# A state-space layer on one core: carried products split by real and imaginary part, states kept in the scan's rows

## The chip, the cores and the metric

The kernel runs on one core of a Trainium2 chip. The metric is device time in microseconds (us) of one execution, lower is better. TensorE (PE in the profile) does the matrix products, VectorE (DVE) and ScalarE (ACT) the work on elements, GpSimd (POOL) some element work and the issue of part of the DMAs, and SyncE's queue (SPq) issues the loads of weights and tables.

## The reference

A trunk of two layers on 256 tokens of 2048 channels in float32: a convolution module, an MLP, a state-space layer with a gated output, a second MLP, a final norm. The change is in the state-space layer. It has 128 groups of 16 channels, each with 64 complex states:

```
bu_re = jnp.einsum("blgc,gpc->blgp", u, bb_re)     # input to the 64 states of each group
bu_im = jnp.einsum("blgc,gpc->blgp", u, bb_im)
_, _, s_re, s_im = lax.associative_scan(combine, (a_re, a_im, bu_re, bu_im), axis=1)
y = (jnp.einsum("blgp,gcp->blgc", s_re, c_re) - jnp.einsum("blgp,gcp->blgc", s_im, c_im))
y = gelu(y + d_skip * h)
z = y @ w_glu                                       # then val * sigmoid(gate)
```

## The kernel before

Nearly all the time is the five large dense products, in which every weight is split into a high and a low part: ScalarE writes `hi` (line 118), VectorE `lo` (line 125, on GpSimd for some steps), and TensorE does three products of each (lines 199 to 234). One step loads a block of weights (`raw`, line 92, on SyncE's queue, in the order of the steps), splits it in two halves up to four halves ahead, and multiplies. A half of the gated output's product is 12 matmuls of 512 columns.

The state-space layer is worked in chunks of 8 tokens. Four blocks B of 512 channels (32 groups) pass through these stages, for each block:

- `ssm_front` and `ssm_turn` (lines 1242 to 1272): products of the chunk's inputs with table W, and a transpose, so that the scan's rows are 128: 64 states of an even group (rows 0 to 63) and of the odd group beside it (rows 64 to 127).
- `ssm_scan` and `ssm_forth` (lines 1274 to 1310): on VectorE, turn the complex recurrence into two real scans, scan over the 32 chunks, and multiply by the turning factors R, which leaves four products in `S`.
- `ssm_states` (lines 1312 to 1320): the four products become the states `SS`, real part in rows 0 to 63 and imaginary part in rows 64 to 127, four VectorE operations on 64 rows each, since the halves change rows.
- `ssm_local` (lines 1322 to 1336): products with table M for what a chunk's own tokens give, `mv` in PSUM. Each matmul gives 32 of the 128 output rows (chunks of one quarter q), so four matmuls of four quarters stand beside each other in the array.
- `ssm_carry` (lines 1338 to 1351): products with table V (128 rows by 128 columns for each group) add what the state at a chunk's start gives: 32 matmuls a block, each of which runs as two instructions in the profile. ScalarE's Gelu then writes `y`.
- `ssm_out` (lines 1353 to 1366): transposes of `y` and the split into `yT`, the operand of the gated output's product.

Block 0 has all of this ahead of the first matmul of the gated output's product (`begin` in `glu`); blocks 1 to 3 are hung on steps of that product by a table of step numbers (`todo`), so their products stand between its matmuls on TensorE, and their VectorE work between the splits. The first block's parts of `ssm_local` for block 1 stand on both sides of `ssm_out(0)`.

Table V is made long before, as background work in the first MLP: `vstage(k)` (lines 1091 to 1105) makes it for 8 groups on VectorE in one buffer `bv` and stores it with one DMA on GpSimd's queue to `Vd` in DRAM; `kstage(k)` makes table K from the same buffer and stores it with four DMAs, `mstage` spreads K to M. `table` (lines 1183 to 1193) later fetches V of one block in two DMAs of 16 groups each, on SyncE's queue, in the order of the weight loads (`before_load`). Instructions of each engine are put into order by a scheduler with a model of its own; anchors (`behind`) fix some of that order.

Of the kernel before, what the change touches and what calls it, by code (L numbers as in the profile page):

```python
# [18 lines left out]
P = 128  # L19
# [8 lines left out]
G, ST, GC = 128, 64, 16  # L28
CH = 8
VW = PAD + T + 2  # L30
NQ = 4
# [5 lines left out]
class Trunk:  # L37
# [823 lines left out]
    def ssm_prep(self):  # L861
        nc, a, bg = self.nc, self.a, self.bg
# [2 lines left out]
        self.Wd = self.dram.tile([P, G, P], F32, name="Wd")  # L865
        self.Kd = self.dram.tile([G, GC, 15 * GC], F32, name="Kd")
        self.Md = self.dram.tile([P, G, P], F32, name="Md")
        self.Vd = self.dram.tile([P, G, P], F32, name="Vd")
        self.Bd = self.dram.tile([G, 2, ST, GC], F32, name="Bd")
        self.Rd = self.dram.tile([P, NQ, 1024], F32, name="Rd")  # L870
        self.xs = self.dram.tile([T, D], F32, name="xs")
        dma = nc.gpsimd.dma_start
# [221 lines left out]
        def vstage(k):  # L1094
            vs = s["bv"][:, 1, 0:1152].rearrange("p (g d c) -> p g d c", d=9, c=GC)
            g = slice(8 * k, 8 * k + 8)
            c = [s["c12"][:, i, g, :].unsqueeze(2).broadcast_to([P, 8, 8, GC]) for i in range(2)]
            p = [s[x][:, g, :].unsqueeze(3).broadcast_to([P, 8, 8, GC]) for x in ("pr", "pi")]
            t = self.t4([P, 8, 8, GC], name="vt")
            v = vs[:, :, 1:9, :]  # L1100
            self.tt(v, c[0], p[0], ALU.mult)
            self.tt(t, c[1], p[1], ALU.mult)
            self.tt(v, v, t, ALU.add)
            nc.scalar.activation(vs[:, :, 0, :], s["c12"][:, 0, g, :], AF.Copy)
            dma(out=self.Vd[:, g, :], in_=v.rearrange("p g d c -> p g (d c)"))

        def kstage(k):
            vs = s["bv"][:, 1, 0:1152].rearrange("p (g x) -> p g x", x=9 * GC)
# [74 lines left out]
    def table(self, kind, B):  # L1183

        if kind == "R":
            t = self.t4([P, 2, 16, 32], name="R") if B != 2 else self.S[:, 1]
            self.fetch(t.rearrange("p i g j -> p (i g j)"), self.Rd[:, B])
        else:
            t = self.blk_tile([P, 32, P], name=kind + "t")
            src = {"W": self.Wd, "M": self.Md, "V": self.Vd}[kind]  # L1190
            for h in range(0, 32, 16):
                self.fetch(t[:, h:h + 16, :], src[:, 32 * B + h:32 * B + h + 16, :])
        self.tables[kind, B] = t

    def ssm_block(self, b):
# [79 lines left out]
    def ssm_scan(self, B, first=None):  # L1275

        nc = self.nc
        ps, R = self.X.pop(B), self.tables["R", B]
        S, t = self.S[:, 0], self.S[:, 2:4]
        m = self.t2([P, 16, 32], name="m")  # L1280
        with self.behind(self.pow_ins):
            nc.gpsimd.memset(m[:, :, 0], 0.0)
        with self.behind(self.xev0 if B == 0 else self.uev):
            nc.scalar.activation(m[:, :, 1:32], self.m8[:, 16 * B:16 * B + 16].unsqueeze(2).broadcast_to([P, 16, 31]), AF.Copy)
        ps = [p.rearrange("p g q j -> p q g j")[:, :, :, 0:31] for p in ps]
        re = lambda x: x.rearrange("p (q g) j -> p q g j", q=NQ)[:, :, :, 1:32]
        c, s = re(R[:, 0]), re(R[:, 1])
        t1, t2 = re(t[:, 0, 0]), re(t[:, 1, 0])
        self.tt(re(S[:, 0]), c, ps[0], ALU.mult)
        self.tt(t1, s, ps[1], ALU.mult)  # L1290
        self.tt(re(S[:, 1]), c, ps[1], ALU.mult)
        self.tt(t2, s, ps[0], ALU.mult)
        self.tt(re(S[:, 0]), re(S[:, 0]), t1, ALU.add)
        self.tt(re(S[:, 1]), re(S[:, 1]), t2, ALU.subtract)
        flat = lambda x: x.rearrange("p g j -> p (g j)")
# [16 lines left out]
    def ssm_states(self, B):  # L1312
        nc = self.nc
        t = self.S[:, 2:4]
        SS = self.t4([P, 16, 2, 32], name="SS")
        for h in range(2):
            r = slice(64 * h, 64 * h + 64)
            self.tt(SS[0:64, :, h, :], t[r, 0, 0], t[r, 1, 1], ALU.subtract)
            self.scaled = nc.vector.tensor_tensor(out=SS[64:128, :, h, :], in0=t[r, 0, 1], in1=t[r, 1, 0], op=ALU.add)
        self.SS[B] = SS  # L1320

    def ssm_local(self, B, g0=0, g1=8):

        nc = self.nc
        M = self.tables["M", B]
        if B == 0:
            A = self.mv[B] = [self.bank([P, 4, CH, GC], name="mv"),
                              self.acc2()[:, 0].rearrange("p (g t c) -> p g t c", g=4, c=GC)]
        else:
            A = self.mv.setdefault(B, [])  # L1330
            A.extend(self.bank([P, 4, CH, GC], name="mv") for _ in range(g0 // 4, g1 // 4))
        U = self.xJ[:, B]
        for g in range(g0, g1):
            for q in range(NQ):
                self.mmm = nc.tensor.matmul(A[g // 4][32 * q:32 * q + 32, g % 4], lhsT=U[:, g, 32 * q:32 * q + 32],
                                 rhs=M[:, 8 * q + g, :], start=g % 4 == 0, stop=False, skip_group_check=True)

    def ssm_carry(self, B):

        nc = self.nc  # L1340
        SS = self.SS.pop(B)
        V = self.tables.pop(("V", B))
        A = self.mv.pop(B)
        for g in (0, 2, 4, 6, 1, 3, 5, 7):
            for q in range(NQ):
                self.vmm = nc.tensor.matmul(A[g // 4][32 * q:32 * q + 32, g % 4], lhsT=SS[:, 4 * q + g // 2, g % 2, :],
                                            rhs=V[:, 8 * q + g, :], start=False, stop=g % 4 == 3, skip_group_check=True)
        y = self.y = self.t4([P, CH, 8, GC], name="y")
        for g, t in (((0, slice(0, CH)), (4, slice(0, CH // 2)), (4, slice(CH // 2, CH))) if B == 0 else
                     ((0, slice(0, CH)), (4, slice(0, CH)))):  # L1350
            nc.scalar.activation(y[:, t, g:g + 4, :].rearrange("p t g c -> p g t c"), A[g // 4][:, :, t], AF.Gelu_apprx_tanh)

    def ssm_out(self, B):
        nc = self.nc
# [12 lines left out]
    def glu(self):  # L1367
# [6 lines left out]
        def begin():  # L1374
            self.mv, self.SS = {}, {}
            self.ssm_start()
# [231 lines left out]
```

## Time and profile before

| | us |
|---|---|
| time, median of 3 runs | 1987.38 (1987.24 to 1987.9) |
| profiled execution | 1987.61 |
| its span, first to last instruction | 1985.8 |
| TensorE busy | 1966.9 (99%) |
| VectorE busy | 1401.3 (71%) |
| ScalarE busy | 952.4 (48%) |
| GpSimd busy | 274.8 (14%) |
| granted TensorE clock, mean | 0.999 of full speed (2.4 GHz) |

The profiled execution is 0.23 us above the median, and 1.8 us of it lie outside the span. The share of busy time says that TensorE sets the time nearly everywhere; what another engine costs is found in the few places where TensorE waits, and what a change of TensorE's own work costs shows wherever it doesn't.

### The profile page before, as it was taken

How to read it: one execution, taken by the hardware profiler on the slowest of the kernel's cores; microseconds unless marked ns; L12 is line 12 of the kernel's file. 1: busy time of each engine (PE TensorE's matmuls, PEld its weight loads, DVE VectorE, ACT ScalarE, POOL GpSimd, SP SyncE). 2: the span in 40 equal slices, each digit the busy share in tenths (PEclk: the TensorE clock that was granted, in tenths of full speed). 3: DMA queues.
4: the chain of work that ended last, by engine and by line, in shares of the span. 5: the costliest groups of instructions: out<-in, count | busy, mean ns of one | idle time of the engine just before them, and what ended most of it. 6: DMA issues, size and time to landing. Idle time of an engine off the chain costs nothing.

```text
span 1985.8 us, 28885 instructions
## 1 busy us (share of the span) xinstructions
PE 1966.9 (99%) x11604; PEld 1687.0 (85%) x11604; DVE 1401.3 (71%) x1904; ACT 952.4 (48%) x1179; POOL 274.8 (14%) x252
## 2 busy tenths in 40 slices
PE   8999999999999999999999999999999999999998
PEld 8999788888888888888888788888888888888887
DVE  6899798888787777777558847565555565555655
ACT  6443655544444544444445445454444454444444
POOL 3998300000000221222010000000000000000000
PEclk9999999999999999999999999999999999999999
DMA  8767458667686877877898865665666656565653
GB/s 228 190 184 207 147 183 267 206 226 245 200 260 192 214 229 253 265 246 238 319 308 298 304 215 186 191 191 189 193 190 192 190 191 191 190 213 190 192 191 128
DMA packets 317030, 428.49 MB, mean 216 GB/s; under 512 B 9761, under 2 KB 211553, under 8 KB 313537
## 3 DMA queue, kind: packets, MB, share of 16 engines
q1 hardware_dynamic: 300976, 384.59, 61.6%
q0 software_dynamic: 12352, 37.49, 6.3%
q10 hardware_dynamic: 3568, 4.56, 0.8%
q8 instruction: 91, 1.49, 0.3%
q14 instruction: 43, 0.35, 0.1%
HBM read 400.08 MB, written 34.91 MB: 219 GB/s over the span
## 4 chain that ended last, share of the span: by engine, by line
PE 96%; DVE 2%; DMA 1%; issue 0%; SPq 0%; POOL 0%; ACT 0%; POOLq 0%; DVEq 0%; ACTq 0%
PE acc L199 24%; PE acc L222 15%; PE acc L223 15%; PE acc L224 15%; PE acc L202 12%; PE acc L213 3%; PE acc L212 3%; PE acc L211 3%; PE pk L484 1%; DMA Vt<-Vd 0%; SPq L92 0%; PE kp L1113 0%; PE xw L1254 0%; DMA raw<-in_conv_w_in_dram 0%; PE xt L254 0%
## 5 line engine op out<-in xcount | busy, mean ns | idle before, releaser
L118 ACT ACTIVATE hi<-raw 128x1024 fp32r<-128x1024 f32 x672 | 711.6, 1060 | 953.5 <-PE acc L224 510.2
L125 DVE TENSOR_TENSOR lo<-raw,hi 128x1024 fp32r<-128x1024 f32 x611 | 747.9, 1226 | 505.6 <-ACT hi L118 501.3
L199 PE MATMUL acc<-hT,hi 128*128 128x512 f32 x2048 | 514.4, 393 | 0.0
L199 PEld LDWEIGHTS acc<-hT,hi 128*128 128x128 f32 x2048 | 368.9, 189 | 68.0 <-issue 1.6
L222 PE MATMUL acc<-hi,rT 128*128 128x512 f32 x992 | 387.2, 391 | 0.0
L223 PE MATMUL acc<-lo,rT 128*128 128x512 f32 x992 | 386.4, 390 | 0.0
L224 PE MATMUL acc<-hi,rT 128*128 128x512 f32 x992 | 386.0, 389 | 0.0
L202 PEld LDWEIGHTS acc<-hT,lo 128*128 128x128 f32 x2048 | 279.6, 190 | 20.0
L202 PE MATMUL acc<-hT,lo 128*128 128x256 f32 x2048 | 286.3, 282 | 0.0
L222 PEld LDWEIGHTS acc<-hi,rT 128*128 128x128 f32 x992 | 186.3, 188 | 39.6 <-issue 1.6
L224 PEld LDWEIGHTS acc<-hi,rT 128*128 128x128 f32 x992 | 186.3, 188 | 39.1
L223 PEld LDWEIGHTS acc<-lo,rT 128*128 128x128 f32 x992 | 186.3, 188 | 38.0 <-issue 0.2
L125 POOL TENSOR_TENSOR lo<-raw,hi 128x1024 fp32r<-128x1024 f32 x60 | 143.1, 2402 | 31.3 <-ACT hi L118 24.8
L211 PE MATMUL acc<-hT,hi 128*128 128x256 f32 x512 | 146.1, 286 | 0.9 <-ACT hi L118 0.9
L212 PE MATMUL acc<-hT,hi 128*128 128x256 f32 x512 | 145.7, 286 | 0.3 <-DVE hT L259 0.3
L213 PE MATMUL acc<-hT,lo 128*128 128x256 f32 x512 | 145.5, 286 | 0.0
L829 DVE SCALAR_TENSOR_TENSOR cv<-vT,dw,cv 128x256 f32<-128x256 f32 x348 | 141.3, 486 | 2.2 <-ACT cv L527 1.7
L820 DVE TENSOR_TENSOR x<-x,acc 128x1024 f32<-128x1024 f32 (+1 forms) x72 | 83.6, 1161 | 27.6 <-PE acc L224 22.0
L211 PEld LDWEIGHTS acc<-hT,hi 128*128 128x128 f32 x512 | 98.9, 193 | 3.0 <-issue 1.6
L222 PE MATMUL acc<-hi,yT 128*128 128x512 f32 x256 | 101.1, 395 | 0.0
L212 PEld LDWEIGHTS acc<-hT,hi 128*128 128x128 f32 x512 | 98.8, 193 | 2.2 <-issue 1.6
L223 PE MATMUL acc<-lo,yT 128*128 128x512 f32 x256 | 99.9, 390 | 0.6 <-DVE lo L125 0.6
(285 smaller groups left out, 1722.9 us busy)
## 6 DMA issues: line engine op xcount, KB each, us to landing
raw<-in_mlp_w_up_dram SPq DMA_DIRECT2D x128, 1024.0 KB, 5.8
raw<-in_mlp_w_down_dram SPq DMA_DIRECT2D x128, 1024.0 KB, 5.2
raw<-in_ssm_w_glu_dram SPq DMA_DIRECT2D x32, 1024.0 KB, 5.5
raw<-in_conv_w_in_dram SPq DMA_DIRECT2D x60, 512.0 KB, 5.6
raw<-in_conv_w_out_dram SPq DMA_DIRECT2D x16, 1024.0 KB, 5.2
Vd<-bv POOLq DMA_DIRECT2D x16, 512.0 KB, 6.3
Md<-Kd POOLq DMA_DIRECT2D x32, 256.0 KB, 7.2
Wt<-Wd SPq DMA_DIRECT2D x8, 1024.0 KB, 10.1
```

The source lines that it names most:

```text
L118: self.nc.scalar.activation(hi, sl, AF.Copy)
L125: ins = eng.tensor_tensor(out=lo, in0=sl, in1=hi.bitcast(F32), op=ALU.subtract)
L199: mm(accs[m], lhsT=hi[:, kk, cs[m]], rhs=xT(k0 + kk), start=first and kk == 0, stop=False)
L202: mm(accs[m][:, 0:T], lhsT=lo[:, kk, cs[m]], rhs=xT(k0 + kk)[:, 0, :], start=False, stop=last and kk == 3)
L211: mm(accs[m], lhsT=hi[:, kk, c], rhs=x[:, 0, :], start=first and kk == 0, stop=False)
L212: mm(accs[m], lhsT=hi[:, kk, c], rhs=x[:, 1, :], start=False, stop=False)
L213: mm(accs[m], lhsT=lo[:, kk, c], rhs=x[:, 0, :], start=False, stop=last and kk == 3)
L222: mm(acc[:, b, :], lhsT=ak[:, 0, t], rhs=hi[:, kk, :], start=first and kk == 0, stop=False)
L223: mm(acc[:, b, :], lhsT=ak[:, 0, t], rhs=lo[:, kk, :], start=False, stop=False)
L224: self.mm_last = mm(acc[:, b, :], lhsT=ak[:, 1, t], rhs=hi[:, kk, :], start=False, stop=last and kk == 1)
L820: return self.nc.vector.tensor_tensor(out=out, in0=a, in1=b, op=op)
L829: return self.nc.vector.scalar_tensor_tensor(out=out, in0=a, scalar=s, in1=b, op0=op0, op1=op1)
```

## The change

- `ssm_states`: two VectorE operations on 128 rows in place of four on 64 rows. The states stay in the scan's rows: even groups in rows 0 to 63, odd groups in rows 64 to 127; `SS[:, 0]` is the real part, `SS[:, 1]` the imaginary part.
- `ssm_carry`: for each group and quarter two matmuls of 64 rows, one with the real and one with the imaginary part, in place of one of 128 rows: 64 matmuls a block. First the real products, even and odd groups in turn, then the imaginary ones, the four even groups and after them the four odd ones.
- Banks by parity: the even groups of a block accumulate in one PSUM bank and the odd ones in the other (before: groups 0 to 3 and 4 to 7). `ssm_local` walks the groups in that order, and each Gelu writes every second group of `y`.
- Table V is stored in these rows: `Vd` has, for each block, the real and the imaginary half, and `vstage` stores 8 groups with four DMAs of 64 rows by 4 groups. `table` fetches the real half with the first DMA and the imaginary half with the second.

```diff
-        self.Vd = self.dram.tile([P, G, P], F32, name="Vd")
+        self.Vd = self.dram.tile([P, NQ, 2, 16, P], F32, name="Vd")
...
-            dma(out=self.Vd[:, g, :], in_=v.rearrange("p g d c -> p g (d c)"))
+            for h in range(2):
+                for i in range(2):
+                    dma(out=self.Vd[64 * h:64 * h + 64, k // NQ, i, 4 * (k % NQ):4 * (k % NQ) + 4, :],
+                        in_=v[64 * i:64 * i + 64, h::2].rearrange("p g d c -> p g (d c)"))
...
-            src = {"W": self.Wd, "M": self.Md, "V": self.Vd}[kind]
             for h in range(0, 32, 16):
-                self.fetch(t[:, h:h + 16, :], src[:, 32 * B + h:32 * B + h + 16, :])
+                src = self.Vd[:, B, h // 16] if kind == "V" else {"W": self.Wd, "M": self.Md}[kind][:, 32 * B + h:32 * B + h + 16, :]
+                self.fetch(t[:, h:h + 16, :], src)
...
-        SS = self.t4([P, 16, 2, 32], name="SS")
-        for h in range(2):
-            r = slice(64 * h, 64 * h + 64)
-            self.tt(SS[0:64, :, h, :], t[r, 0, 0], t[r, 1, 1], ALU.subtract)
-            self.scaled = nc.vector.tensor_tensor(out=SS[64:128, :, h, :], in0=t[r, 0, 1], in1=t[r, 1, 0], op=ALU.add)
+        SS = self.t4([P, 2, 16, 32], name="SS")
+        self.tt(SS[:, 0], t[:, 0, 0], t[:, 1, 1], ALU.subtract)
+        self.scaled = nc.vector.tensor_tensor(out=SS[:, 1], in0=t[:, 0, 1], in1=t[:, 1, 0], op=ALU.add)
...
+    def ssm_group(self, A, i):
+        g = 2 * (i % 4) + i // 4
+        return g, A[i // 4][:, i % 4]
...
-        for g in (0, 2, 4, 6, 1, 3, 5, 7):
-            for q in range(NQ):
-                self.vmm = nc.tensor.matmul(A[g // 4][32 * q:32 * q + 32, g % 4], lhsT=SS[:, 4 * q + g // 2, g % 2, :],
-                                            rhs=V[:, 8 * q + g, :], start=False, stop=g % 4 == 3, skip_group_check=True)
...
+        def products(part, i):
+            g, out = self.ssm_group(A, i)
+            r = slice(64 * (g % 2), 64 * (g % 2) + 64)
             for q in range(NQ):
+                k = 4 * q + g // 2
+                self.vmm = nc.tensor.matmul(out[32 * q:32 * q + 32], lhsT=SS[r, part, k, :], rhs=V[r, 16 * part + k, :],
+                                            start=False, stop=part == 1 and i % 4 == 3, skip_group_check=True)
+        for i in (0, 4, 1, 5, 2, 6, 3, 7):
+            products(0, i)
+        for i in range(8):
+            products(1, i)
```

TensorE at block 0's carried products. Before, from the second pass over the two banks on (the pair of rows at the top stands twice); `mv` and `acc` are the two banks, x8 are matmuls:

```order
L1346 MATMUL mv_9958<-Vt_9448,SS_10045 32x128 x8
L1346 MATMUL acc_9959<-Vt_9448,SS_10045 32x128 x8
L1335 MATMUL mv_10086<-Mt_9946,xJ_9516 32x128 x16
L1359 MATMUL yt_10104<-ident_95,y_10082 128x128 x4
L1359 MATMUL yt_10105<-ident_95,y_10082 128x128 x4
```

The same place of the changed kernel (the pair of x4 rows at the top stands four times: these are the real products):

```order
L1358 MATMUL mv_10006<-Vt_9496,SS_10093 32x128 x4
L1358 MATMUL acc_10007<-Vt_9496,SS_10093 32x128 x4
L1358 MATMUL mv_10006<-Vt_9496,SS_10093 32x128 x16
L1358 MATMUL acc_10007<-Vt_9496,SS_10093 32x128 x16
L1342 MATMUL mv_10164<-Mt_9994,xJ_9564 32x128 x16
L1374 MATMUL yt_10182<-ident_95,y_10096 128x128 x4
```

Nothing moves past anything here: 32 matmuls on two banks by fours, then 32 that fill one bank after the other, stand where 32 stood.

VectorE at block 1's states, between `ssm_forth(1)` and the splits of the gated output's weights (`lo`) and the scaling of block 2's inputs (`xJ`). Before (the pair of `SS` rows stands twice):

```order
L820 TENSOR_TENSOR SS_10148<-S_9846 64x16x32
L1319 TENSOR_TENSOR SS_10148<-S_9846 64x16x32
L125 TENSOR_TENSOR lo_10154<-raw_9698,hi_10153 128x1024
L125 TENSOR_TENSOR lo_10174<-raw_9749,hi_10173 128x1024
L820 TENSOR_TENSOR xJ_9516<-xJ_9516,rJ_9839 128x512 x2
L125 TENSOR_TENSOR lo_10192<-raw_9749,hi_10191 128x1024
```

Now:

```order
L820 TENSOR_TENSOR SS_10226<-S_9894 128x512
L1320 TENSOR_TENSOR SS_10226<-S_9894 128x512
L125 TENSOR_TENSOR lo_10230<-raw_9746,hi_10229 128x1024
L820 TENSOR_TENSOR xJ_9564<-xJ_9564,rJ_9887 128x512 x2
L125 TENSOR_TENSOR lo_10250<-raw_9797,hi_10249 128x1024
L125 TENSOR_TENSOR lo_10268<-raw_9797,hi_10267 128x1024
```

Two operations are gone, and the scaling of block 2 stands ahead of one split more.

GpSimd's queue in the first MLP, at the stores of tables V and K. Before:

```order
L1105 DMA Vd<-bv 128x8x128 x2
L1121 DMA Kd<-ks 16x2x128 x8
L1124 DMA Md<-Kd 16x32x128 x7
L1105 DMA Vd<-bv 128x8x128
L1124 DMA Md<-Kd 16x32x128
```

Now:

```order
L1107 DMA Vd<-bv 64x4x128 x8
L1124 DMA Kd<-ks 16x2x128 x8
L1127 DMA Md<-Kd 16x32x128 x6
L1107 DMA Vd<-bv 64x4x128 x4
L1127 DMA Md<-Kd 16x32x128 x2
```

Each store of V has become four; the order of the rest differs by one row. Around this place VectorE's background operations stand one to three rows from where they stood, among the same splits.

## Rows read from the trace of the kernel before

**Rows 1.** Page, part 1: busy us, share of the span, instructions of each engine.

```profile
PE 1966.9 (99%) x11604; PEld 1687.0 (85%) x11604; DVE 1401.3 (71%) x1904; ACT 952.4 (48%) x1179; POOL 274.8 (14%) x252
```

**Rows 2.** Waits of TensorE, whole span: waiter, releaser, us in total, times, longest.

```profile
PE mv L1346 <- DVE SS L1319: 1.9, 2, 1.5
PE xtr L1271 <- ACT X L1257: 0.7, 2, 0.3
PE mv L1346 <- DMA Vt<-Vd: 0.6, 1, 0.6
PE acc L223 <- DVE lo L125: 0.6, 1, 0.6
```

**Rows 3.** Busy time by stretch, background stage: us, then busy us of each engine.

```profile
650.00:1000.00 350.00, 350.00 (x1970) 293.88 (x1969) 254.33 (x281) 163.05 (x204) 73.90 (x116) 1.00 0.81 255
```

**Rows 4.** Chain that ended last, block 0: start us, us, what.

```profile
1063.62 1.01 PE warm L189 x8
...
1064.68 0.68 DVE SS L820
...
1066.81 0.70 DVE SS L1319
...
1067.55 0.65 PE mv L1346 x16
1068.20 0.44 PE acc L1346 x16
...
1071.54 0.43 PE acc L222
1071.98 0.24 PE acc L223
```

**Rows 5.** Timeline of block 0: start, us, engine line op, [idle before].

```profile
1066.11 0.65 PE L1346 MATMUL mv<-Vt,SS 128*32 128x128 f32 x16 [1.50 <-DVE SS L1319]
...
1068.45 1.06 PE L1335 MATMUL mv<-Mt,xJ 128*32 128x128 f32 x32
1068.76 0.66 ACT L1351 ACTIVATE y<-acc 128x256 f32<-128x256 f32 x2
```

**Rows 6.** Groups by shape, VectorE: count, then busy us, mean ns, idle before.

```profile
L1319 DVE TENSOR_TENSOR SS<-S 64x512 f32<-64x512 f32 x8 | 5.5, 687 | 0.1
...
L820 DVE TENSOR_TENSOR xJ<-xJ,rJ 128x512 f32<-128x512 f32 x6 | 3.9, 686 | 0.1
```

**Rows 7.** Chain that ended last, block 1's carried products.

```profile
1079.98 1.89 PE mv L1346 x64
```

**Rows 8.** Timeline of TensorE: eight small products of 32 columns.

```profile
259.22 0.31 PE L907 MATMUL dgp<-ident,dg 128*32 128x32 f32 x8
```

**Rows 9.** Chain that ended last, ahead of block 3's carried products.

```profile
1138.15 0.69 DVE SS L1319
...
1138.87 1.24 DVE lo L125
...
1141.09 9.55 DMA Vt<-Vd
```

**Rows 10.** Timeline of ScalarE, the same place.

```profile
1136.54 1.06 ACT L118 ACTIVATE hi<-raw 128x1024 fp32r<-128x1024 f32 x1 [1.66 <-PE acc L224]
```

**Rows 11.** Chain that ended last, ahead of TensorE's wait for a split.

```profile
1091.04 1.07 ACT hi L118
```

**Rows 12.** Timeline of GpSimd in the background stage.

```profile
815.76 2.03 POOL L1121 DMA_DIRECT2D Kd<-ks  x4 [6.78 <-DVE ks L829]
823.50 0.93 POOL L1105 DMA_DIRECT2D Vd<-bv  x1 [5.71 <-DVE bv L820]
...
936.01 5.02 POOL L1124 DMA_DIRECT2D Md<-Kd  x8 [1.91 <-DMA Kd<-ks]
```

**Rows 13.** Timeline of VectorE: the next writing of that buffer.

```profile
831.18 1.22 DVE L820 TENSOR_TENSOR bv<-c,pv 128x1024 f32<-128x1024 f32 x1
```

**Rows 14.** Timeline of SyncE's queue: the first fetch of table M.

```profile
986.10 0.86 SPq L92 DMA_DIRECT2D Mt<-Md  x2
```

More of the change, by code (lines that the diff above doesn't have):

```diff
@@ L1292, in ssm_scan @@
         self.tt(t2, s, ps[0], ALU.mult)
+        flat = lambda x: x.rearrange("p g j -> p (g j)")
         self.tt(re(S[:, 0]), re(S[:, 0]), t1, ALU.add)
         self.tt(re(S[:, 1]), re(S[:, 1]), t2, ALU.subtract)
-        flat = lambda x: x.rearrange("p g j -> p (g j)")
         with self.behind(first) if first is not None else nullcontext():
@@ L1314, in ssm_states, with ssm_local @@
         t = self.S[:, 2:4]
-        SS = self.t4([P, 16, 2, 32], name="SS")
-        for h in range(2):
-            r = slice(64 * h, 64 * h + 64)
-            self.tt(SS[0:64, :, h, :], t[r, 0, 0], t[r, 1, 1], ALU.subtract)
-            self.scaled = nc.vector.tensor_tensor(out=SS[64:128, :, h, :], in0=t[r, 0, 1], in1=t[r, 1, 0], op=ALU.add)
+        SS = self.t4([P, 2, 16, 32], name="SS")
+        self.tt(SS[:, 0], t[:, 0, 0], t[:, 1, 1], ALU.subtract)
+        self.scaled = nc.vector.tensor_tensor(out=SS[:, 1], in0=t[:, 0, 1], in1=t[:, 1, 0], op=ALU.add)
         self.SS[B] = SS
-    def ssm_local(self, B, g0=0, g1=8):
+    def ssm_group(self, A, i):
+        g = 2 * (i % 4) + i // 4
+        return g, A[i // 4][:, i % 4]
+    def ssm_local(self, B, i0=0, i1=8):
         nc = self.nc
@@ L1330, in ssm_local @@
             A = self.mv.setdefault(B, [])
-            A.extend(self.bank([P, 4, CH, GC], name="mv") for _ in range(g0 // 4, g1 // 4))
+            A.extend(self.bank([P, 4, CH, GC], name="mv") for _ in range(len(A), (i1 + 3) // 4))
         U = self.xJ[:, B]
-        for g in range(g0, g1):
+        for i in range(i0, i1):
+            g, out = self.ssm_group(A, i)
             for q in range(NQ):
-                self.mmm = nc.tensor.matmul(A[g // 4][32 * q:32 * q + 32, g % 4], lhsT=U[:, g, 32 * q:32 * q + 32],
-                                 rhs=M[:, 8 * q + g, :], start=g % 4 == 0, stop=False, skip_group_check=True)
+                self.mmm = nc.tensor.matmul(out[32 * q:32 * q + 32], lhsT=U[:, g, 32 * q:32 * q + 32],
+                                 rhs=M[:, 8 * q + g, :], start=i % 4 == 0, stop=False, skip_group_check=True)
     def ssm_carry(self, B):
@@ L1343, in ssm_carry @@
         A = self.mv.pop(B)
-        for g in (0, 2, 4, 6, 1, 3, 5, 7):
+        y = self.y = self.t4([P, CH, 8, GC], name="y")
+        def products(part, i):
+            g, out = self.ssm_group(A, i)
+            r = slice(64 * (g % 2), 64 * (g % 2) + 64)
             for q in range(NQ):
-                self.vmm = nc.tensor.matmul(A[g // 4][32 * q:32 * q + 32, g % 4], lhsT=SS[:, 4 * q + g // 2, g % 2, :],
-                                            rhs=V[:, 8 * q + g, :], start=False, stop=g % 4 == 3, skip_group_check=True)
[L1348 to L1351, printed above, removed]
+                k = 4 * q + g // 2
[5 more added lines that the diff above has]
+            products(1, i)
+        for h in range(2):
+            for t in (slice(0, CH // 2), slice(CH // 2, CH)) if B == 0 and h else (slice(0, CH),):
+                nc.scalar.activation(y[:, t, h::2, :].rearrange("p t g c -> p g t c"), A[h][:, :, t], AF.Gelu_apprx_tanh)
     def ssm_out(self, B):
```

## The prediction

> **What bounds the kernel now.** I read the page's busy shares first: TensorE is busy for 1966.9 of 1985.8 us [rows 1], so the question everywhere is whether TensorE waits. The waits of TensorE over the whole span answer it: beside the start, only four lines bear on the state-space layer [rows 2]. TensorE waited 1.9 us in two pieces for `SS` (block 0's states), 0.6 us once for the fetch of table V (block 3), 0.6 us once for a split `lo`, and 0.7 us for `X`, which the change doesn't touch. From 650 to 1000 us, where table V is made, TensorE was busy for all of 350.00 us [rows 3]: work added there on other engines costs nothing as long as it doesn't hold up a split. So the change can win back 1.9 + 0.6 + 0.6 = 3.1 us at the very most, and every product that it adds to TensorE outside those waits is paid in full.
>
> **Block 0, the one place where the states are on the path.** The chain there runs over VectorE: four `SS` operations from 1064.68 to 1067.51, then products [rows 4]. The first pair of operations releases 32 of the products at 1066.11, 0.05 us after its end [rows 5]; the rest come after 1067.55, and the next products, of `ssm_local(1)`, begin at 1068.45 [rows 5]. An operation of 64 rows by 512 takes 687 ns and one of 128 rows by 512 takes 686 [rows 6]: rows are free on VectorE, columns are not. So two operations replace four at the same price each, and block 0's states end 1.38 us earlier, at about 1066.1; the real part is there at 1064.68 + 0.68 = 1065.36, and the real products can begin at 1065.41.
>
> What the products cost is the open question. A block's 64 instructions (32 matmuls) take 1.89 us [rows 7], 30 ns each; within a run 16 of them take 0.44 us [rows 4], so four that stand beside each other, one for each quarter, are one step of 0.11 us. Eight products that fill the whole array take 1.01 us, 126 ns each [rows 4]: products with 32 output rows do run four abreast. The change makes 128 instructions of 64 rows, 32 steps of four. No row of this trace shows products on half the rows, so I bound it. If the two row halves don't run beside each other, a block takes 32 steps, 3.5 us, 1.76 us more. If they do, the real products (even and odd groups in turn, on different rows and different banks) take 8 steps, 0.88 us. The imaginary products go through four even groups and then four odd ones, so neighbours want the same rows: 16 steps with one overlap where odd follows even, 1.65 us. That is 2.53 us for a block in place of 1.76, 0.8 more; a real part that pairs badly (the second instruction of a matmul held behind the first) costs about two steps more, 1.0. I take 1.0 us for the real part and 2.65 for the block, 0.9 more than before, since the row of the same engine that is nearest, products four abreast, shows the array taken in parts at full rate.
>
> The Trainium skill speaks against a shorter price for half the rows: in "TensorE: Matmul & The Clock Gate" (section "Why this matters for your kernels") a matmul of few rows takes the same time as one of 128, and the gain is only in tiles that run concurrently. No run here shows it yet; by that rule the imaginary part alone costs what the whole product cost, as in the sum above.
>
> Block 0 then goes: real products 1065.41 to 1066.41 (the imaginary states are there at 1066.1, so no second wait), imaginary ones to 1068.06, and a change of the array's shape before `ssm_local(1)`, which before had the same shape as the carried products. The product after such a change took 0.43 us in place of 0.24 [rows 4], so I add 0.15: 1068.2 against 1068.45, **0.25 us won**. Both ends: 8 steps for the real part give 0.4 won; no overlap gives 1065.41 + 3.5 + 0.15 = 1069.1, 0.65 lost. Gelu doesn't spoil it: the even bank is complete at about 1067.3, and the odd bank's two halves take 0.66 [rows 5] after 1068.2, while `ssm_local(1)` keeps TensorE for 1.0 us. Where the 1.38 us go: TensorE's two waits, 1.9 us together [rows 2], become one of about 0.8, and most of the difference is refilled with products. VectorE gets ahead by the rest, and nothing there waits for it, since the splits of `yT` hang on TensorE's transposes.
>
> **Blocks 1 to 3.** Their states are ready before their products' turn, so the earlier states bring nothing directly, and the products stand between matmuls of the gated output, where TensorE never rests. Each costs its 0.9 us: **2.7 us lost** (bounds 2.3, and 5.3 without overlap).
>
> **Block 3's table.** TensorE waited 0.6 us for V [rows 2]. The fetch was issued at 1141.09 and took 9.55 us; it stood on SyncE's queue behind a load of weights that waited for the split ending at 1140.1, which stood on VectorE behind block 3's four `SS` operations [rows 9]. With 1.38 us less there, that split can begin when `hi` is ready, at 1136.54 + 1.06 = 1137.6 [rows 10] and not 1138.87: the whole row moves up 1.25 us, more than the wait, and the real products need only the first of the two fetches. **0.64 us won** (0.0 if the fetch gets slower by as much). Late next there is nothing but TensorE's own work.
>
> **The wait for a split near 1105** (0.6 us [rows 2]) I leave in place. Its chain begins at 1091.04 with a `hi` that waits for TensorE to free a buffer [rows 11], after block 1's states, and runs through the scan and `ssm_forth` of block 2, which the change doesn't shorten; more products of block 1 ahead of it shift its start and its end alike. That VectorE scales block 2's inputs one split earlier changes nothing between those two points.
>
> **Table V in the background.** 16 stores on GpSimd's queue become 64. A store of 512 KB took GpSimd 0.93 us, four small ones of K took 2.03 us [rows 12], 0.51 each; four of 128 KB lie between, so 2.0 to 3.7 us in place of 0.93, I take 2.4, 24 us over the 16 stages. GpSimd is busy for 73.90 of 350 us there [rows 3]. Its queue waits for VectorE and not the reverse; behind V's stores stand those of K and M, and M's last issue ended at 941 us while its first fetch is at 986.10 [rows 12, 14]: 45 us of cover. The tighter cover is the buffer: the next stage's first operation may write it only when all four stores have read it. The closest pair: the store issued at 823.50, the next writing at 831.18 [rows 12, 13], 7.7 us. If the last of four lands 1.5 us later, VectorE may wait about that long once or twice, with splits queued behind it; they are made up to four halves ahead, and a half is 12 matmuls of 0.24 us, 2.8 us. Cost nothing; uncovered, 1 to 2 us at each of one or two places.
>
> **Sum.** -0.25 + 2.7 - 0.64 = +1.8 us. The profiled execution (1987.61) is 0.23 above the median of 1987.38; the sum is a difference and goes on the median: **1989.2 us**, own range 1988.2 to 1990.4. A measurement of this kernel can tell about 0.2% from no change, 4.0 us, so this counts as no change.
>
> **The rivals.**
>
> *No overlap of row halves* (ends slower). For: no row shows it, and both halves send their sums to the same output rows, though to different banks. Against: four column parts run abreast at full rate. It decides in the real part: if a block's 64 real instructions take 1.8 us and not about 1.0, then +0.65 + 5.3 - 0.64 = +5.3, 1992.7 us.
>
> *A floor between starts.* Eight small products with 32 columns took 0.31 us in all [rows 8], one alone about 0.23: their starts lie within 0.08 us, some 11 ns apart, so issue isn't what limits real products at 15 ns. The Trainium skill says otherwise ("TensorE: Matmul & The Clock Gate", section "Wait — 56ns, not 53.3ns?": starts never come closer than about 25 ns); this trace disagrees at 11 ns. If the mechanism held for these products at a spacing near the 27 ns of a step today (0.44 us for 16), the real part would take about 1.7 us, a block 1.5 to 1.6 more: +0.5 + 4.7 - 0.64 = +4.5, 1991.9 us.
>
> *The stores hold up VectorE.* For: 7.7 us of cover against a slower landing. Against: TensorE has no wait at all in that stretch. If one or two splits come late beyond the four halves: 1.8 + 1 to 4, about 1991.5.
>
> *Cheaper than I think* (imaginary products overlap too, or the change does on TensorE what its words suggest: two halves for the price of one). A block then costs 0.1 more: -0.9 in block 0 + 0.3 - 0.64 = -1.2, 1986.1 us; with the wait near 1105 gone too, 1985.5. Faster by over 4 us is out of reach, since all the waits together are 3.1.
>
> **How the numbers follow.** Forecast 0.68, no overlap 0.16, floor 0.05, stores 0.05, cheaper 0.06. Slower by over 0.2% (above 1991.4): 0.16 + 0.03 + 0.02, with a little of the forecast's own tail, 0.22; faster 0.01; within, 0.77. The range that leaves out no more than 2 in 10 takes in the forecast, most of the cheaper case and the end without overlap: 1986.5 to 1992.7.
>
> **What would show it.** `SS` as two operations of about 0.69 us in each block, the real products starting at the first one's end; block 0's `ssm_local(1)` beginning about 0.25 us earlier. The 128 instructions of blocks 1 to 3 taking about 2.8 us in place of 1.89 in the chain: 3.6 would be the first rival, 2.0 the last. TensorE's waits: about 0.8 us for `SS` in one piece, none for `Vt`, the 0.6 for `lo` still there. Stretch 650 to 1000 us still without a gap on TensorE. The prediction is wrong if the halves don't overlap, or if TensorE waits anywhere that it didn't before.

## The result, and the profile after

The changed kernel takes 1992.31 us (median of 9 runs, 1991.44 to 1993.65); the kernel before took 1987.38 (9 runs, 1986.95 to 1988.87) beside it. The ratio is 1.0025, with a 95% interval of 1.0016 to 1.0033: slower by about a quarter of a per cent, just over what this kernel's measurement can tell from no change. The forecast was 1989.2. The profiled execution took 1993.37 us with a span of 1991.6, 5.8 us more than the span before, and the rest of this section is about those 5.8. That execution lies 1.06 us above its median and the one of before 0.23 above, so the medians are 4.9 us apart and the traces 5.8.

TensorE's waits over the whole span of the changed kernel (waiter, releaser, us in total, times, longest):

```profile
PE mv L1342 <- issue: 3.3, 1, 3.3
...
PE mv L1358 <- DVE SS L820: 0.8, 1, 0.8
PE xtr L1274 <- ACT X L1260: 0.7, 2, 0.4
PE acc L223 <- DVE lo L125: 0.6, 1, 0.6
```

Against [rows 2], the waits for the states have gone from 1.9 to 0.8 us in one piece, the one for table V is gone, and the one for `lo` is still there. All of that was forecast. The first line was not: TensorE stood for 3.3 us in the middle of `ssm_local(1)` (line 1342), and the releaser "issue" says that the profile shows nothing it waited for, no engine and no data. Such a standstill is called a stop below.

The chain that ended last, around block 0 (start us, us, what), against [rows 4]:

```profile
1064.65 0.70 DVE SS L820
1065.40 0.31 PE mv L1358 x4
...
1066.55 0.48 PE mv L1358 x20
1067.03 0.05 PE acc L1358 x4
1067.08 0.06 PE mv L1358 x4
...
1067.36 0.49 PE acc L1358 x20
1067.85 0.57 PE mv L1342 x14
1068.41 3.29 issue
1071.71 1.44 PE mv L1342 x18
1073.14 1.90 PE yt L1374 x8
1075.04 1.87 PE mv L1342 x32
1076.91 0.70 PE acc L222
...
1085.56 2.38 PE mv L1358 x128
```

The carried products start as the first of two `SS` operations ends and are through at 1067.85, 0.8 us ahead of the kernel before (0.67 by the starts of what follows). Then 14 of the 32 products of a half of `ssm_local(1)` run, and TensorE stands. When it goes on, work that took 1.02 us before (the eight transposes, `yt`) takes 1.90, and 32 local products take 1.87 where they took 1.01. The busy times by stretch show the other half of the loss (us, then busy us of PE, PEld, DVE, ACT, POOL with instructions; the granted clock, DMA share, GB/s):

```profile
1060.00:1070.60 10.60, 7.60 (x226) 6.56 (x219) 9.27 (x12) 6.36 (x12) 0.13 (x1) 1.00 1.01 420
1070.60:1077.50 6.90, 5.79 (x60) 4.46 (x60) 2.48 (x4) 1.20 (x2) 0.00 (x0) 0.51 0.97 385
1077.50:1085.00 7.50, 7.50 (x35) 6.20 (x34) 7.43 (x10) 2.13 (x2) 0.00 (x0) 1.00 0.07 20
```

The granted clock was at its lower level, 1.2 in place of 2.4 GHz, from 1070.6 to 1077.5, from shortly before the end of the stop. In the first stretch the DMA engines were full, at 420 GB/s.

At block 3 a row of the kernel before, which does not stand above, belongs beside its counterpart. Timeline of TensorE (start us, us, operation, [idle before <- releaser]), before:

```profile
1149.42 0.63 PE L1346 MATMUL mv<-Vt,SS 128*32 128x128 f32 x8
1150.69 1.94 PE L1346 MATMUL mv<-Vt,SS 128*32 128x128 f32 x56 [0.64 <-DMA Vt<-Vd]
```

and after:

```profile
1155.94 2.45 PE L1358 MATMUL mv<-Vt,SS 64*32 64x128 f32 x128
```

Before, the 64 products needed 3.14 us from their start to the next instruction (at 1152.56), 1.26 more than in a block without a wait, and not 0.64 more: eight products had started when the table was late, and their modelled ends cover the first part of the standstill. After, 128 products run through in 2.38 us from their start to the next one's (2.45 with the modelled end of the last). The fetches of the table on SyncE's queue, before and after:

```profile
1140.58 0.93 SPq L92 DMA_DIRECT2D Vt<-Vd  x2
1145.87 0.93 SPq L92 DMA_DIRECT2D Vt<-Vd  x2
```

Now the ledger, from the starts of TensorE's runs in both traces. Up to the carried products the two kernels stand within 0.03 us of each other. Start of `ssm_local(1)`: 0.67 us ahead (1067.78 against 1068.45). `ssm_local(1)` and the transposes between its halves: 9.06 us where they took 3.02, 6.04 lost, 3.6 of it the standstill from start to start and the rest the low clock. Gated output behind it: 0.21 lost. Carried products of blocks 1 and 2: 2.38 in place of 1.88 and 1.91, 0.97 lost together. Block 3: 2.38 in place of 3.14, 0.76 won. Sum -0.67 + 6.04 + 0.21 + 0.97 - 0.76 = +5.79; the last matmul is 5.77 us later. So the parts that the prediction priced come to about -0.5 us, and the whole loss is the stop and what follows from it.

What was asked of the profile elsewhere holds. VectorE's groups by shape (count, busy us, mean ns, idle before), GpSimd's timeline at one of V's stages, and the stretch 650 to 1000 us:

```profile
L820 DVE TENSOR_TENSOR SS<-S 128x512 f32<-128x512 f32 x4 | 2.8, 688 | 0.2
L1320 DVE TENSOR_TENSOR SS<-S 128x512 f32<-128x512 f32 x4 | 2.7, 684 | 0.0
```

```profile
828.20 2.48 POOL L1107 DMA_DIRECT2D Vd<-bv  x4 [10.48 <-DVE bv L820]
```

```profile
650.00:1000.00 350.00, 350.00 (x1970) 293.72 (x1969) 253.87 (x281) 163.00 (x204) 98.84 (x164) 1.00 0.81 255
```

GpSimd is busy 24.9 us longer there (73.90 in [rows 3]), and TensorE still has no gap.

### The profile page after: what moved, and what is told of

It reads as the page before. It is cut to its first block, busy times and chain, and to the rows that moved or that the text cites. A ratio compares the mean times of both kernels' runs of the same rounds, so it can differ in the third digit from the quotient of the medians.

```text
span 1991.6 us, 29457 instructions
## 1 busy us (share of the span) xinstructions
PE 1970.9 (99%) x11860; PEld 1689.6 (85%) x11860; DVE 1394.0 (70%) x1896; ACT 952.4 (48%) x1179; POOL 299.9 (15%) x300
## 4 chain that ended last, share of the span: by engine, by line
PE 97%; DVE 1%; issue 1%; SPq 0%; DMA 0%; ACT 0%; POOL 0%; POOLq 0%; DVEq 0%; ACTq 0%
PE acc L199 24%; PE acc L222 16%; PE acc L223 15%; PE acc L224 15%; PE acc L202 12%; PE acc L212 3%; PE acc L211 3%; PE acc L213 3%; PE pk L484 1%; PE kp L1116 0%; PE mv L1342 0%; PE mv L1358 0%; SPq L92 0%; PE xw L1257 0%; DMA raw<-in_conv_w_in_dram 0%
```

## Where a stop with no releaser comes from

**Theory A: TensorE ran out of instructions.** The profile's table of DMA queues has one that carries instructions (queue, kind: packets, MB, share), and its size gives away whose they are:

```profile
PE 1970.9 (99%) x11860; PEld 1689.6 (85%) x11860; DVE 1394.0 (70%) x1896; ACT 952.4 (48%) x1179; POOL 299.9 (15%) x300
...
q8 instruction: 93, 1.52, 0.3%
```

TensorE has 11,860 matmuls and as many weight loads, 23,720 instructions. The 93 packets of queue 8 are 16,384 bytes each in the trace; if they are TensorE's, one brings 23,720 / 93 = 255 instructions of 64 bytes. The other kernels confirm it. All records of TensorE in the trace, its own waits included, are 23,342 in the kernel before, 23,726 in run 4 below and 23,856 in the changed kernel; a 256th of these is 91.2, 92.7 and 93.2, and queue 8 brought 91, 92 and 93 packets. Before, and run 4:

```profile
q8 instruction: 91, 1.49, 0.3%
q8 instruction: 92, 1.51, 0.3%
```

In the trace of the changed kernel the packet that matters started at 1069.24 and took 1.03 us; narrow windows bracket it, with no row of queue 8 from 1067.5 to 1069.2 and this one from 1069.2 to 1070.3:

```profile
q8 instruction: 1, 0.02, 5.9%
```

TensorE went on at 1071.71, 1.44 us after the packet had come. By theory A a packet of 256 is asked for at a fixed count of instructions, the request queues behind whatever the DMA engines are doing (here the loads of tables and weights), and the change is at fault because 128 carried products with their weight loads are 256 instructions, a whole packet, in 2.4 us. In the kernel before the same packet started at 1069.81 and ended at 1070.82; with the same 1.4 us behind it the instructions were there at about 1072.2, and the instruction at which the changed kernel stopped has its like at 1072.77 there. It had about half a microsecond to spare, and nothing in its waits shows that. How late the packet is can be counted: in the kernel before, 89 of the 91 packets start when TensorE has begun between 152 and 230 records of a stretch of 256, but this one at 364; in the changed kernel it is at 449, and there TensorE had none left.

The Trainium skill, "Advanced Engine Details and Errata" (section "ISA Cache"), says that instructions are cached in lines of 16 KB, which hold 256 instructions. The trace agrees as to the size: 16,384 bytes a packet.

**Rivals.** B: the stop comes from the new products themselves (64 rows on two banks in quick turn). C: it comes from the place in the program or from so much work at once, whatever the count. In what was expected of runs 1 to 4, C is another rival: that the local products wait for table M. The first four runs stood beside 31 runs of the kernel before with a median of 1987.7, runs 5 to 7 and the last beside 27 and 15 with 1987.75 and 1987.64, runs 8 and 9 beside 19 with 1987.69.

### 1. Hold back the loads of table W

```diff
+            if hold is not None:
+                self.nc.gpsimd.tensor_copy(out=t[:, 0, 0:GC], in_=hold)
...
-            get("W", 2)
-            get("R", 2)
             self.ssm_forth(0, self.ssm_scan(0))
             self.ssm_states(0)
+            held = self.SS[0][:, 1, 0, 0:GC]
+            get("W", 2, held)
+            get("R", 2)
```

> The changed kernel, but the fetch of block 2's table W, and all loads queued behind it, wait on GpSimd for block 0's states (one small copy reads them and writes into the table's tile). Theory A (TensorE runs out of instructions in block 0, because the fetch of the next page of them comes late behind the burst of table loads, and 64 more matmuls use up what is there): the instruction fetch comes before 1068 us, the 3.3 us stop in the second block's local products is gone and with it the half clock; time 1986 to 1988 us. Theory B (the stop belongs to the change from 64-row to 128-row products): the stop stays, 1991 to 1993. Theory C (the local products wait for table M): M is fetched as before but with less beside it, the stop gets shorter by the same as M's landing, 1988 to 1992.

Measured: 1991.71 us, ratio 1.0018 (1.0009 to 1.0027). The stop became 2.7 us, at the same instruction; the packet started at 1068.70.

```profile
PE mv L1344 <- issue: 2.7, 1, 2.7
```

A miss: theory A had 1986 to 1988 us and no stop, and the time lies where theory B had it. The loads of V(1) and of other tables ahead of W were still on the DMA engines; that this took away too little is an argument. The intervals of the two kernels overlap, so all that the run gives is one trace in which the packet comes earlier and the stop is shorter.

### 2. Hold back table V(1) as well

```diff
-            get("V", 1)
...
             self.ssm_states(0)
+            held = self.SS[0][:, 1, 0, 0:GC]
+            get("V", 1, held)
+            get("W", 2)
+            get("R", 2)
```

> As the kernel that holds W of block 2, but block 1's table V is held too. Theory A: fewer loads beside the instruction fetch, no stop, 1986 to 1988 us unless V of block 1 now comes late for its products near 1079 (then up to 1 us more). Theory B: the stop stays, 1991 to 1993. Theory C: as for the other.

Measured: 1989.17 us, ratio 1.0008 (0.9999 to 1.0018). TensorE's waits:

```profile
PE mv L1344 <- issue: 0.4, 1, 0.4
...
PE yt L1376 <- ACT y L1368: 0.8, 1, 0.8
```

The stop is 0.4 us, the clock stays at its upper level, and the packet started at 1067.13, 0.9 us after the carried products began (1066.21), against 3.8 us in the changed kernel. So traffic on the DMA engines delays the packet. The second row is the price: the chain to that wait, near 1086, runs over a load of weights that took 14.28 us from 1070.60 on, so this is no cure, and the time is above the 1986 to 1988 us expected.

### 3. The kernel before, with small products ahead of block 0

```diff
             self.keep_warm(4, self.ut)
+            ps = self.bank([P, 32], name="more")
+            with self.behind(self.ut):
+                for n in range(32):
+                    q = n % NQ
+                    nc.tensor.matmul(ps[32 * q:32 * q + 32], lhsT=self.ident[:, 0:32], rhs=self.ident[:, 0:32],
+                                     start=True, stop=True, skip_group_check=True)
```

> The kernel before, with 32 small matmuls (32 by 32 columns, whose result nobody reads) in block 0 where TensorE waits for the states anyway: 64 more instructions and as many weight loads, as many as the change adds in block 0, with no product on 64 rows. They take about 0.7 of 1.5 us of waiting. Theory A: TensorE stops for 2 to 4 us in the local products or just behind, with half clock after it, 1990 to 1993 us. Theories B and C: no stop, 1987.2 to 1987.8.

Measured: 1988.98 us, ratio 1.0004 (0.9995 to 1.0013). The chain that ended last shows the stop in a kernel that has no product of 64 rows:

```profile
1068.08 0.65 PE mv L1346 x16
1068.72 0.44 PE acc L1346 x16
1069.16 0.43 PE mv L1335 x14
1069.59 0.94 issue
```

Rival B falls. The size was missed: a stop of 0.9 us and no time at the lower clock, where theory A had 2 to 4 us and 1990 to 1993 us. But the place agrees with a count: in the changed kernel TensorE stopped 128 + 14 = 142 matmuls after the start of block 0's carried products, here after 64 + 14 = 78, which is 64 fewer, and 64 is what the 32 small products add (each is two matmul instructions). Counted in the trace's records from the start (TensorE's own waits among them), both stops come after 13,505 instructions, which is 51 packets of 256 and the 449 of above; the packet that comes late is the 52nd in both.

### 4. Block 0 in its old form, blocks 1 to 3 in the new

```diff
+        if B == 0:
+            for g in (0, 2, 4, 6, 1, 3, 5, 7):
+                for q in range(NQ):
+                    self.vmm = nc.tensor.matmul(A[g // 4][32 * q:32 * q + 32, g % 4], lhsT=SS[:, 4 * q + g // 2, g % 2, :],
+                                                rhs=V[:, 8 * q + g, :], start=False, stop=g % 4 == 3, skip_group_check=True)
```

The states and the store of V for block 0 are in the old form too.

> The changed kernel with block 0 in the form of before (four operations for its states, 32 matmuls of 128 rows, its table V stored and fetched as before); blocks 1 to 3 as changed. All theories: no stop in block 0. It measures the rest: three times 2.38 in place of 1.88 us for the carried products (+1.5), the wait for block 3's table V gone (-0.6 to -0.8): 1988.0 to 1988.4 us. If the stop came from anything in blocks 1 to 3 or in the stores of V, it would stay and the time would be above 1991.

Measured: 1988.98 us, ratio 1.0006 (0.9997 to 1.0016). No stop; `SS` is waited for as in the kernel before, and the carried products of blocks 1 to 3 take what they take in the changed kernel:

```profile
PE mv L1375 <- DVE SS L1325: 1.9, 2, 1.5
```

```profile
1080.29 2.38 PE mv L1370 x128
```

So in the changed kernel the stop hangs on block 0's new form, and the new products of the other blocks cost the same without it. The starts of TensorE's runs give the terms again: +0.50 and +0.47 in blocks 1 and 2, -0.76 in block 3. This run was 0.3 us late before block 0 began, and lost 0.36 in the gated output behind block 2, which I didn't follow up; the median is some 1 us above what the terms alone give, and 0.6 above the range expected.

### 5. The changed kernel, with the count shifted

```diff
-        self.keep_warm(6, self.mm_last)
+        self.keep_warm(2, self.mm_last)
+        ps = self.bank([P, 32], name="more")
+        with self.behind(self.mm_last):
+            for i in range(20):
+                q = i % NQ
+                nc.tensor.matmul(ps[32 * q:32 * q + 32], lhsT=self.ident[:, 0:32], rhs=self.ident[:, 0:32],
+                                 start=True, stop=True, skip_group_check=True)
```

> The changed kernel, with 20 small products of 32 rows and 32 columns (their results are read by nobody) and 4 fewer warming steps ahead of block 0, together 64 more instructions for TensorE before the carried products of block 0; nothing else is altered. Theory A (the stop of 3.3 us in the local half of block 1 is TensorE waiting for its own instructions, asked for at a fixed count that in the changed kernel is crossed as the 128 carried products begin): the count is now crossed some 4 us earlier, in idle time, so the stop and the half clock behind it are gone, and the time is 1986.4 to 1987.6 us, 0.2 us or more under the kernel before at the middle. Rival C (the stop comes from the place in the program or from the heat of so many products at once, whatever the count): the stop stays at 2.5 to 3.5 us and the time is 1991 to 1993 us.

Measured: 1987.53 us, ratio 0.9999 (0.9990 to 1.0008). The chain around block 0:

```profile
1064.35 0.70 DVE SS L820
...
1067.55 1.01 PE mv L1348 x32
1068.56 1.02 PE yt L1380 x8
1069.58 1.01 PE mv L1348 x32
1070.59 0.44 PE acc L222
```

The stop is gone, the clock stays up, and all that comes from 64 more instructions that compute nothing, some 15 us ahead of the carried products. The packet started at 1063.85, ahead of the carried products and not behind them. Rival C falls: the place and the work are the same. From the end of the wait for the first `SS` on, everything runs as the terms say, but for block 3, whose products took 2.56 us and not 2.38 in this trace.

### 6. Both parts alternating

```diff
-        for i in range(8):
+        for i in (0, 4, 1, 5, 2, 6, 3, 7):
             products(1, i)
```

On top of run 5.

> As the kernel with the shifted count, and besides the carried products of the imaginary part also go by alternating halves of the rows, as those of the real part do (group 0, 4, 1, 5 and so on). If the halves overlap whenever neighbouring products use different rows, the 128 products of a block take about 1.9 to 2.1 us and not 2.38, which is 0.3 to 0.5 us in each of four blocks: 1985.0 to 1986.3 us. If the imaginary part already overlapped as far as its waits allow, there is no difference from the kernel with the shifted count. A further possibility: faster consumption of instructions brings a stop at another block, which would show as issue time of 0.5 us or more in a local half.

Measured: 1986.27 us, ratio 0.9992 (0.9983 to 1.0001).

```profile
1079.32 1.96 PE mv L1364 x128
```

The 128 products of blocks 1 to 3 take 1.96 to 1.98 us and not 2.38, nearly the 1.88 of the 64 whole ones (block 0: 2.10). No stop appears elsewhere.

### 7. The control: the kernel before, with the count shifted

The edit of run 5, on the kernel before.

> Control: the kernel before with the same 64 more instructions ahead of block 0. By theory A the kernel before had its instructions in time by some 0.4 us, so nothing is won or lost: 1987.2 to 1988.2 us. If the shift by itself is worth something (the small products warm the clock, say), it shows here as 0.5 us or more.

Measured: 1987.64 us, ratio 0.9999 (0.9990 to 1.0008). The shift alone is worth nothing.

### 8. No alternating at all

```diff
-        for i in (0, 4, 1, 5, 2, 6, 3, 7):
+        for i in range(8):
             products(0, i)
```

On top of run 5.

> The kernel with the shifted count, whose products of the real part no longer alternate between the halves of the rows: four groups of one half, then four of the other, as the imaginary part has them. If neighbouring products overlap only when they use different rows, the real part of each block now takes as long as the imaginary part did (about 1.4 us where it took 0.95), the 128 products of a block take 2.8 to 2.9 us and not 2.38, and the time is 4 x 0.45 = 1.8 us above the kernel with the shifted count: 1988.8 to 1989.8 us. If the order makes no difference and every product is as short by its size alone, the carry stays at 2.4 us and the time at 1987.5 us. If nothing overlapped without the alternating, the carry would take 0.95 + 1.88 us or more in each part, up to 3.8 us, and the time would be 1992 us or more.

Measured: 1988.80 us, ratio 1.0004 (0.9995 to 1.0013), some 1.3 us above run 5.

```profile
1080.01 2.71 PE mv L1364 x128
```

Order matters, as expected, though in block 1 by 0.33 us and not 0.45. The three orders make a series there: 2.71 us with neither part alternating, 2.38 with one, 1.96 with both. Even the first is far from the 3.8 us of no overlap at all. The starts show why, as in the chain of block 0 above: in the changed kernel's imaginary part 20 products of the even half start, then odd and even ones by fours in turn, 12 of each, then 20 of the odd half. Where the half changes, three steps of each run beside each other; the others still go four every 0.11 us. In all these orders the PSUM bank changes with the half of the rows, so what is due to the one and what to the other isn't separated.

### 9. Half the shift

Eight small products and all six warming steps, 32 more instructions in place of 64.

> The changed kernel with 8 small products ahead of block 0 (32 more instructions, half the shift of the run before; all warming steps kept; nobody reads their results). By theory A the count at which the instructions are asked for is crossed about 2.1 us earlier than in the changed kernel (at the start of the warming steps, and not at the start of the carried products), and the place where TensorE has none left comes about 0.5 us earlier, so the stop should be 3.3 - 2.1 + 0.5 = 1.7 us (1.2 to 2.2), at the same count of instructions and so 16 products earlier in the program, with less or no time at half clock, and a time of 1988.3 to 1990.3 us. If the stop is a matter of being there or not whatever the count, it is 3.3 us or zero: 1992 or 1987.5 us.

Measured: 1990.70 us, ratio 1.0012 (1.0002 to 1.0022). The chain:

```profile
1066.44 0.48 PE mv L1364 x20
1067.24 0.48 PE acc L1364 x18
1067.72 2.57 issue
1070.29 0.38 PE acc L1364 x2
```

The stop has moved into the carried products, two before their end: 126 matmuls after their start, 16 fewer than the 142 of the changed kernel, and 16 is what the eight small products add. That is the count of 13,505 for the third time, and among products that read nothing of table M. The size missed: 2.6 us, where 1.7 was expected from a request that comes 2.1 us earlier, and the time is 0.4 us above the range. The size isn't the same each time: in 6 of the ten runs the mean granted clock is 0.998 (1990.69 to 1992.33 us), in 4 it is 0.999 (1989.05 to 1989.93), and the one traced (1991.52) is of the longer kind. I had put the request at a count worked out from the spacing of packets; it isn't recorded. If it stands at a count that this run still reaches only with the carried products (TensorE rests at 13,251 before them here, and at 13,282 in runs 5 and 6), the half shift moves nothing but the place, which is what is seen. That is an inference, and the packet's varying delay would do as well. Against it: in quiet stretches of the same traces packets start as early as 152 records into their 256, which would be 13,208 here, below every one of these counts.

### 10. Run 6 once more

> The kernel with the shifted count and both parts alternating once more, unaltered, since its interval of 0.9983 to 1.0001 left open whether it beats the kernel before. From the first time, 1986.2 to 1986.8 us and a ratio of 0.999 to 0.9996 are expected; a ratio of 1.000 or more would mean that the first run's lead was chance.

Measured: 1986.05 us, ratio 0.9990 (0.9981 to 0.9999). With the first time (1986.27) that is a lead of about 1.5 us, 0.1%: below what counts as a difference for this kernel, yet in both comparisons the best version of all that ran. The time is 0.15 us under the range expected, the ratio at its end. In this trace block 3's products waited 0.3 us for table V again and took 2.58 us, so that wait isn't gone in every run.

Across the runs with a stop, the packet's end and TensorE's next matmul keep their distance: 1.44 us in the changed kernel, 1.46 in run 1, 1.38 in run 2, 1.28 in run 3, 1.39 in run 9, while the stops themselves go from 0.4 to 3.3 us. That, the fixed count, and the cure by instructions that do nothing are why I take theory A as shown. What sets the delay between request and packet beyond the traffic stays open.

The mean granted clock of every single run adds how often the clock fell. It is 0.998 in all 9 runs of the changed kernel, in 8 of 10 of run 1 and 6 of 10 of run 9; in runs 2, 3, 5, 6, 8 and 10 it is 0.999 throughout. The kernel before, timed beside runs 1 to 10, has 0.998 in 13 of its 92 (1988.59 to 1989.97 us), run 4 in 2 of 10 and run 7 in 1 of 11. So the kernel before may now and then use up its half microsecond too; none of those executions has a trace, so that is not shown.

## Why the prediction came out as it did

**The direction and the size.** The forecast was no change, with a sum of +1.8 us; it came out 4.9 us above, inside the range, close to the 1992.7 of "no overlap of row halves", but not for that rival's reason. Its point of decision was whether the real part's 64 instructions take 1.8 us or about 1.0. They took 0.90 from start to start (eight every 0.11 us), so the rival is out, and the agreement of the numbers is chance. The sum's own range, 1988.2 to 1990.4, missed; the wide one reached so far up only for this rival's sake, so to lie inside it is luck. By its last sign of being wrong, a wait of TensorE where there was none before, the prediction was wrong.

**The step that failed** is none of the terms. It is the sentence that 3.1 us of waits are all there is to win and that every added product "is paid in full" at its own length: instructions also have to be brought. The change put 256 instructions of TensorE where 128 stood, at a place where the DMA engines were full, and the sum had no term for that: +6.25 us (6.04 and 0.21). The prediction named the case in its last words only ("if TensorE waits anywhere that it didn't before"), without a mechanism or a price. The profile had the clue: a queue of kind "instruction" in its third part, whose packets times 256 make TensorE's count.

**Block 0.** Forecast -0.25, measured -0.67. The mechanism was right: the real products start at the first operation's end and a single wait of 0.8 us is left. The 128 instructions took 2.38 us where 2.65 was taken, because the real part did better (0.90 against 1.0) and the imaginary one overlaps for three steps where the half changes, not for one (1.48 against 1.65). Those 2.38 hold what there is of the 0.15 for a change of the array's shape: 0.20 us lie between the last carried product's start and the next one's, where 0.09 lay before.

**Blocks 1 to 3.** Forecast +0.9 each, measured +0.5 (2.38 against 1.88). This is the same term, mis-sized the same way: I took the imaginary part as 16 steps of 0.11 us with one overlap, 1.65 us, and it took 1.48. In run 6 that part takes 1.06 us with neighbours on different rows; this bears out the reason given (neighbours that want the same rows), though the banks change with the rows.

**Block 3's table.** Forecast -0.64, measured -1.26 (block 3 took 0.76 less in all, although its products cost 0.50 more as in the other blocks). The mechanism held: the fetch began 10.07 us ahead of the products' start (issued at 1145.87, products at 1155.94), where it had 8.84 before (1140.58 and 1149.42): 1.23 us earlier, against the 1.25 of the prediction. The size was read from idle time, and an idle time behind matmuls whose modelled ends reach into the standstill is too short.

**The wait for a split near 1105** stayed at 0.6 us, as forecast. **The stores of V**: 2.48 us for four where 2.4 was taken, 24.9 us in all where 24 was, and no gap on TensorE. **VectorE's price by columns alone**: 684 to 688 ns for 128 rows, as taken.

**The floor between starts** is out: in run 6, 128 products start within 1.96 us, 15 ns apart. The Trainium skill, "TensorE: Matmul & The Clock Gate" (section "Wait — 56ns, not 53.3ns?"), holds that starts don't come closer than about 25 ns; for products on separate parts of the array the trace differs, and it decides.

**The cheaper rival** (1986.1) was nearer to the change's own worth than the forecast: without the stop, run 5 gave 1987.53 beside 1987.75, so -0.2 us, between the rival's -1.2 and the forecast's +1.8. Its price of 0.1 us a block is not that of this change (0.5) but that of both parts alternating (1.96 against 1.88), which gave 1986.27 and 1986.05.

## What to carry to other kernels

A wait of TensorE with no releaser, in a stretch with many short instructions and full DMA engines, is a reason to look at the instruction queue: count matmuls and weight loads from the start to the stop, and see whether a harmless shift of that count moves it. When a change multiplies small instructions, price their supply beside their execution, above all where loads are prefetched at the same time. And read a wait's cost from start to start against an undisturbed block, not from the idle time alone.

## What the runs showed of the hardware

- A packet of the instruction queue that is due while table loads run at about 420 GB/s can come late enough to stop TensorE for 3.3 us; with those loads held back the stop was 0.4 us. TensorE resumes 1.3 to 1.5 us after the packet's end.
- With a stop of 3.3 us, in the changed kernel, went 6.8 us at the lower granted clock (1.2 GHz), from 1.1 us before its end; behind stops of 2.6 and 2.7 us (runs 9 and 1) came 3.4 us each; with stops of 0.9 and 0.4 us (runs 3 and 2) none.
- Products of 64 rows and 32 columns on opposite halves of the rows, and in two PSUM banks, run at once: 128 of them take 1.96 us, 64 of the whole 128 rows 1.88. Grouped by half they take 2.71.
- TensorE's instructions came in packets of 256 on a DMA queue of their own: 91, 92 and 93 packets for 23,342, 23,726 and 23,856 records, and every stop came after 13,505 of them.
